# A weight block's two parts move from a raw buffer to a high-part buffer in a decoder layer on Trainium2

## The chip, the cores and the metric

The kernel runs on one core of one Trainium2 chip. The metric is the device time of one execution in microseconds (us), lower is better; the number given for a kernel is the median of its runs. Engines are named as in the profile: PE (TensorE's matmuls), PEld (its weight loads), DVE (VectorE), ACT (ScalarE), POOL (GpSimd) and SP (SyncE, which issues most DMAs).

## The reference

One layer of a hybrid decoder on 512 tokens of width 1024, in float32: RMSNorm, one input projection, a convolution branch and a gated linear attention branch, their merge, an output projection, then a channel mixer, and a last RMSNorm. The change lies in the channel mixer:

```python
u2 = _rmsnorm(h, norm2_g[l])
z = _causal_dwconv(u2 @ w_ffn_up[l], ffn_dw_w[l], ffn_dw_b[l])
h = h + (jax.nn.silu(z[..., :FFN_DIM]) * z[..., FFN_DIM:]) @ w_ffn_down[l]
```

FFN_DIM is 2816, so `w_ffn_up` is 1024 x 5632: 44 column blocks of 128. Block i (0 to 21) gives the gate of channel group i and block 22+i its value.

## The kernel before

**Three products for one.** Every float32 operand is split into a high part (the value cast to the type that TensorE multiplies, `float32r`) and a low part (the value minus its high part). One product is then three matmuls: low by high, high by low, high by high (`mm3`, L398 to L400, or `col_products`, L409).

**The flow of weights.** `order` lists all weight blocks in the order of their use. `load` (L223 issues the DMA on SP) brings the next block into a buffer of the tag "raw". `split_weight` makes its parts: ACT casts into a buffer of the tag "whi", then DVE subtracts into one of the tag "wlo" (L326 and L327 where operands are built first, L345 and L354 else). For blocks in `ADDED` the low part is made without DVE: ACT writes the negated block (L347) and POOL issues a DMA that adds the block from memory once more (L348). Each of the three tags has four buffers of 128 x 1024 floats. `prefetch(n)` splits up to n blocks ahead of the one in use; each split calls `load` once, so loads run four entries ahead.

**What orders the work.** The kernel is written with a library that plans each engine's queue and the buffers when it is built: each instruction is put into its engine's queue when a model of times has its operands and a buffer ready, earlier program text first, and a buffer passes to the next tile of its tag when the last reader of the former is done. On the chip the queues then run in that fixed order.

**Pairs in the up projection.** Channel groups come in pairs (p, q), in three lists: (0,2) (1,3) (4,6) (5,7), then (8,10) (9,11) (20,21), then (12,14) (13,15) (16,18) (17,19). After each list follows a part of the down projection (`seven("w_down", ...)`). For q in 6, 7, 10, 11, 14, 15 and 18 gate and value of q are computed together, by seven half-width products instead of eight (`up_seven`). Its four weights come from the raw blocks b (gate q) and x (value q): b itself, the sum block called "x" in the order (`up_operand`, L288, a third raw buffer), r1 called "n" and r0's right half called "m". The steps on TensorE are a11 (weight b), s1 (x), n2 (x), a12 (b), n3 (n), s4 (n), a22 (m), each of four `mm3` with 256 columns, twelve matmuls. Between them run the 24 matmuls of p's value block (block 22+p) in lots of three, one lot after a11, s1, n2 and n3, two after a12 and s4; `beside()` does this. Ahead of the pair stands p's gate, 24 matmuls on L409. ACT copies intermediate banks out for later steps: L1581 after a11, which n2 then adds to; L1584 after s1; L1587 after n2, before n3 adds to the bank; L1591 after n3, before a22. DVE forms the other half at L1593 and L1594 after s4. Then p's group goes through its depthwise convolution and gate (L1391, L1393, L1399, L1401) and is split for the down projection (L1406, L1407; L1414, L1424 to L1426 form sums).

Inside `up_seven` the next weights are split in steps: one (the next pair's gate) after n2, one (its value) after a12, one (block b of the next q) after s4, one (block x) after a22; n and m are split when `up_seven` begins.

**The lines of the change.** Block m is only 512 wide, so its high and low part share one buffer of 1024, named `wm`: ACT casts at L319, DVE subtracts at L320. In the kernel before that buffer has the tag "raw".

Of the kernel before, what the change touches and what calls it, by code (L numbers as in the profile page):

```python
# [11 lines left out]
F32R = mybir.dt.float32r  # L12
# [5 lines left out]
P = 128  # L18
D = 1024
# [60 lines left out]
def trunk_layer(ctx: ExitStack, tc: tile.TileContext, a: dict, out: bass.AP):  # L80
    nc = tc.nc

    def pool(name, bufs, space=None):
        kw = {"space": space} if space is not None else {}
        return ctx.enter_context(tc.tile_pool(name=name, bufs=bufs, **kw))
# [8 lines left out]
    wp = pool("weights", 1)  # L94
# [18 lines left out]
    def nm(s):  # L113
        return f"{s}_{next(names)}"

    def heap(dt=F32):
        return hp.tile([P, T], dt, tag="h", name=nm("h"))
# [85 lines left out]
    def load():  # L203
        if len(raws) < len(order):
            name, j = order[len(raws)]
            if name in SEVEN:
                raws.append(load_block(name, *j))
                if name in INNER and raws[-1] is None:
                    load()
                return  # L210
            raw = None
            if name == "w_up7":
                i, s = j
                name, j = "w_up", {"b": i, "x": FT + i}.get(s)
            if name == "w_r0":
                raw = raw_tile()
                for i in range(2):
                    c = slice((2 * j + i) * P, (2 * j + i + 1) * P)
                    dst = raw[:, i * T : (i + 1) * T].rearrange("p (c x) -> p c x", x=P)
                    nc.sync.dma_start(dst, a["w_r"][:4, :, c].rearrange("c p x -> p c x"))  # L220
            elif j is not None:
                raw = raw_tile()
                sent[name, j] = nc.sync.dma_start(raw, a[name.rstrip("0")][j])  # L223
            raws.append(raw)
# [50 lines left out]
    def operand(name, raw, pairs, step, d):  # L275

        if step == "s4":
            return kept[name, pairs, d, "b22"]
        if step == "n2" and name not in INNER:
            nc.vector.tensor_tensor(kept[name, pairs, d], kept[name, pairs, d], raw, ALU.add)  # L280
        return raw if step in ("a12", "n3") else kept[name, pairs, d]

    def up_operand(raw, i, s):

        if s in "bx":
            kept[i, s] = raw
        r0, r1 = kept[i, "b"], kept.get((i, "x"))
        add = lambda engine, dst, x, y: engine.tensor_tensor(dst, x, y, ALU.add)  # L288
        if s == "x":
            both = kept[i, "sum"] = raw_tile()  # L290
            add(nc.vector, both[:, :T], r0[:, :T], r1[:, :T])
            add(nc.vector, both[:, T:], both[:, :T], r1[:, T:])
            add(nc.gpsimd, r1[:, :T], r1[:, :T], r1[:, T:])
            add(nc.gpsimd, r0[:, T:], r0[:, T:], both[:, T:])
        return {"b": r0, "x": kept.get((i, "sum")), "m": r0[:, T:], "n": r1}[s]

    def sum_on(name, pairs, step, d):

        where = {"a11": (0, 1), "n2": (1, 0)}
        if name in INNER:  # L300
            where["s1"] = (1, 1)
            if (step, d) in (("s4", 0), ("s4", 1)):
                add_n3(name, pairs, d)
        if step in where:
            nxt = block(name, pairs, d, *where[step])
            nc.gpsimd.dma_start(kept[name, pairs, d], nxt, accum_op=ALU.add)

    def split_weight(between=None):
        if len(ready) < len(order):
            while len(raws) <= len(ready):  # L310
                load()
            raw = raws[len(ready)]
            name, spec = order[len(ready)]
            if name in SEVEN or name == "w_up7":
                raw = operand(name, raw, *spec) if name in SEVEN else up_operand(raw, *spec)
                n = raw.shape[-1]
                if name == "w_up7" and spec[1] == "m":
                    both = wp.tile([P, D], F32R, tag="raw", name=nm("wm"), bufs=4)
                    nc.scalar.copy(both[:, :T], raw)  # L319
                    nc.vector.tensor_tensor(both[:, T:], raw, both[:, :T].bitcast(F32), ALU.subtract)  # L320
                    ready.append((both[:, :T], both[:, T:]))
                    load()
                    return
                hi = wp.tile([P, D], F32R, tag="whi", name=nm("whi"), bufs=4)[:, :n]
                lo = wp.tile([P, D], F32R, tag="wlo", name=nm("wlo"), bufs=4)[:, :n]
                nc.scalar.copy(hi, raw)  # L326
                pace[0] = nc.vector.tensor_tensor(lo, raw, hi.bitcast(F32), ALU.subtract)  # L327
                if name in SEVEN:
                    sum_on(name, *spec)
                skipped = name in INNER and raws[len(ready)] is None  # L330
                ready.append((hi, lo))
                if not skipped:
                    load()
                return
            hi = wp.tile([P, D], F32R, tag="whi", name=nm("whi"), bufs=4)
            if order[len(ready)][0] == "w_low":
                nc.scalar.copy(hi, raw)
                if order[len(ready)][1] == 0:
                    part_lo = lambda t: t.rearrange("p (k c) -> p k c", c=P)[:, :, :RANK]
                    nc.vector.tensor_tensor(part_lo(hi), part_lo(raw), part_lo(hi.bitcast(F32)), ALU.subtract)  # L340
                ready.append((hi, None))
                load()
                return
            lo = wp.tile([P, D], F32R, tag="wlo", name=nm("wlo"), bufs=4)
            nc.scalar.copy(hi, raw)  # L345
            if order[len(ready)] in ADDED:
                pace[0] = nc.scalar.activation(lo, raw, AF.Copy, scale=-1.0)  # L347
                nc.gpsimd.dma_start(lo, a[name][spec], accum_op=ALU.add)  # L348
                ready.append((hi, lo, (name, spec) in LOW_LAST_IN))
                load()  # L350
                return
            if between:
                between()
            pace[0] = nc.vector.tensor_tensor(lo, raw, hi.bitcast(F32), ALU.subtract)  # L354
            ready.append((hi, lo))
            load()

    def prefetch(n):

        while len(ready) < min(used[0] + n, len(order)):  # L360
            split_weight()
# [821 lines left out]
    def between(h, i):  # L1183
        if h < 2:
            (glu_value if h else glu_gate)(GLU_AT[0] + GLU_AT[1] + i)
        elif h < HEADS:
            gate_b(2 * (h - 2) + i)
        else:
            gate_b(6 + i)
# [68 lines left out]
    for p, q in O_PAIRS:  # L1258

        f1 = merged(p)  # L1260
        both = heap(F32R)
# [471 lines left out]
```

## Time and profile before

| | us |
|---|---|
| median of 3 runs | 824.15 (823.98 to 824.63) |
| the profiled execution's own time | 824.73 |
| its span, first to last instruction | 823.0 |
| PE busy | 812.3 (99%) |
| DVE busy | 675.6 (82%) |
| ACT busy | 471.3 (57%) |
| POOL busy | 122.9 (15%) |

The profile is of one execution. A row of the timeline has the start (us from the span's start), the duration, the engine and source line, and what is written from what by the program's names; in brackets stands the engine's idle time before it and what ended it. Matmuls overlap in the pipeline, so their starts, not their durations, say how fast TensorE goes. A row of the waits has who waited, for whom, the total, the number of times and the longest. A row of the stretches has, after the two times and the length, the busy time of PE, PEld, DVE, ACT and POOL, each with its count, then the granted clock, the DMAs' share and GB/s.

### The profile page before, as it was taken

How to read it: one execution, taken by the hardware profiler on the slowest of the kernel's cores; microseconds unless marked ns; L12 is line 12 of the kernel's file. 1: busy time of each engine (PE TensorE's matmuls, PEld its weight loads, DVE VectorE, ACT ScalarE, POOL GpSimd, SP SyncE). 2: the span in 40 equal slices, each digit the busy share in tenths (PEclk: the TensorE clock that was granted, in tenths of full speed). 3: DMA queues.
4: the chain of work that ended last, by engine and by line, in shares of the span. 5: the costliest groups of instructions: out<-in, count | busy, mean ns of one | idle time of the engine just before them, and what ended most of it. 6: DMA issues, size and time to landing. Idle time of an engine off the chain costs nothing.

```text
span 823.0 us, 11027 instructions
## 1 busy us (share of the span) xinstructions
PE 812.3 (99%) x4090; PEld 689.9 (84%) x4090; DVE 675.6 (82%) x983; ACT 471.3 (57%) x669; POOL 122.9 (15%) x153
## 2 busy tenths in 40 slices
PE   8999999999999999999999999999999999999996
PEld 7988888888888888888888898888788888988885
DVE  6898988999988899845678859689858888588895
ACT  7663547695453552469345759554446543667455
POOL 2021101312121121000011011211021111220111
PEclk9999999999999999999999999999999999999999
DMA  9999859569666678222348459346835646557562
GB/s 328 315 319 234 199 138 225 142 154 222 149 138 143 152 191 191 81 77 79 126 110 214 148 164 222 98 122 154 217 102 149 160 92 215 154 154 203 131 128 102
DMA packets 50213, 136.65 MB, mean 166 GB/s; under 512 B 4624, under 2 KB 17184, under 8 KB 50160
## 3 DMA queue, kind: packets, MB, share of 16 engines
q1 hardware_dynamic: 37456, 90.91, 31.6%
q0 software_dynamic: 12528, 44.83, 31.4%
q8 instruction: 32, 0.52, 0.2%
q10 hardware_dynamic: 176, 0.20, 0.1%
q14 instruction: 21, 0.17, 0.1%
HBM read 133.84 MB, written 6.29 MB: 170 GB/s over the span
## 4 chain that ended last, share of the span: by engine, by line
PE 91%; DMA 3%; DVE 2%; issue 2%; ACT 1%; POOL 0%; POOLq 0%; SPq 0%; DVEq 0%; ACTq 0%
PE mm L409 52%; PE mm L399 8%; PE mm L400 8%; PE mm L398 8%; PE mm L673 2%; PE ax L398 2%; PE ax L399 2%; PE ax L400 2%; DMA wlo<-in_w_glu_dram 1%; PE ax L1147 1%; PE ax L484 1%; DMA raw<-in_w_up_dram 1%; DMA kept<-rows 1%; PE ax L1149 1%; PE ax L1129 1%
## 5 line engine op out<-in xcount | busy, mean ns | idle before, releaser
L409 PE MATMUL mm<-ul,whi 128*128 128x512 f32 (+1 forms) x608 | 226.8, 373 | 0.0
L409 PE MATMUL mm<-uh,whi 128*128 128x512 f32 (+1 forms) x608 | 226.5, 373 | 0.0
L409 PE MATMUL mm<-uh,wlo 128*128 128x512 f32 (+1 forms) x608 | 217.2, 377 | 0.3 <-DMA wlo<-in_w_glu_dram 0.2
L823 DVE SCALAR_TENSOR_TENSOR c<-h,pp,c 128x507 f32<-128x507 f32 (+20 forms) x240 | 169.9, 732 | 3.2 <-ACT c L820 0.3
L409 PEld LDWEIGHTS mm<-uh,whi 128*128 128x128 f32 x608 | 114.5, 188 | 20.4
L409 PEld LDWEIGHTS mm<-uh,wlo 128*128 128x128 f32 x608 | 114.6, 189 | 19.0 <-DMA wlo<-in_w_glu_dram 0.7
L409 PEld LDWEIGHTS mm<-ul,whi 128*128 128x128 f32 x608 | 114.8, 189 | 17.9
L345 ACT CAST whi<-raw 128x1024 fp32r<-128x1024 f32 x94 | 97.4, 1043 | 49.0 <-PE mm L409 32.0
L326 ACT CAST whi<-raw 128x1024 fp32r<-128x1024 f32 (+1 forms) x53 | 54.1, 1027 | 53.0 <-PE mm L400 29.8
L347 ACT ACTIVATE wlo<-raw 128x1024 fp32r<-128x1024 f32 x47 | 49.5, 1058 | 58.8 <-PE mm L409 54.5
L327 DVE TENSOR_TENSOR wlo<-raw,whi 128x1024 fp32r<-128x1024 f32 (+1 forms) x53 | 66.6, 1264 | 11.6 <-ACT whi L326 11.0
L1393 DVE SCALAR_TENSOR_TENSOR tmp<-mm,pp,tmp 128x511 f32<-128x511 f32 (+1 forms) x88 | 64.6, 743 | 13.2 <-ACT tmp L1391 12.8
L354 DVE TENSOR_TENSOR wlo<-raw,whi 128x1024 fp32r<-128x1024 f32 x47 | 57.0, 1220 | 16.0 <-ACT whi L345 15.6
L326 ACT CAST whi<-kept 128x1024 fp32r<-128x1024 f32 (+1 forms) x44 | 44.2, 1009 | 32.7 <-PE mm L400 10.5
L327 DVE TENSOR_TENSOR wlo<-kept,whi 128x1024 fp32r<-128x1024 f32 (+1 forms) x44 | 52.3, 1196 | 5.1 <-ACT whi L326 4.8
L1391 ACT ACTIVATE tmp<-mm,pp 128x512 f32<-128x512 f32 x44 | 33.3, 775 | 11.7 <-PE mm L409 9.7
L409 PE MATMUL mm<-h,whi 128*128 128x512 f32 x128 | 39.4, 389 | 0.0
L1313 DVE TENSOR_TENSOR hres<-hres,mm 128x512 f32<-128x512 f32 (+1 forms) x49 | 32.4, 670 | 2.5 <-PE mm L400 2.3
L348 POOL DMA_DIRECT2D wlo<-in_w_up_dram x18 | 15.6, 866 | 96.9 <-ACT wlo L347 79.0
L409 PEld LDWEIGHTS mm<-h,whi 128*128 128x128 f32 x128 | 24.0, 188 | 5.2 <-issue 0.2
L399 PE MATMUL mm<-wlo,sh 128*128 128x512 f32 x66 | 25.9, 393 | 0.0
L400 PE MATMUL mm<-whi,sh 128*128 128x512 f32 x66 | 25.7, 390 | 0.0
(366 smaller groups left out, 1649.1 us busy)
## 6 DMA issues: line engine op xcount, KB each, us to landing
raw<-in_w_up_dram SPq DMA_DIRECT2D x44, 512.0 KB, 4.6
wlo<-in_w_up_dram POOLq DMA_DIRECT2D x18, 512.0 KB, 7.8
raw<-in_w_glu_dram SPq DMA_DIRECT2D x16, 512.0 KB, 5.6
raw<-in_w_down_dram SPq DMA_DIRECT2D x15, 512.0 KB, 5.2
kept<-in_w_down_dram POOLq DMA_DIRECT2D x10, 512.0 KB, 5.4
raw<-in_w_v_dram SPq DMA_DIRECT2D x8, 512.0 KB, 6.4
rows<-in_w_r_dram SPq DMA_DIRECT2D x16, 256.0 KB, 5.9
raw<-in_w_qk_dram SPq DMA_DIRECT2D x8, 512.0 KB, 4.0
```

The costliest lines, as they stand in the source:

```text
L326: nc.scalar.copy(hi, raw)
L327: pace[0] = nc.vector.tensor_tensor(lo, raw, hi.bitcast(F32), ALU.subtract)
L345: nc.scalar.copy(hi, raw)
L347: pace[0] = nc.scalar.activation(lo, raw, AF.Copy, scale=-1.0)
L354: pace[0] = nc.vector.tensor_tensor(lo, raw, hi.bitcast(F32), ALU.subtract)
L398: nc.tensor.matmul(acc, ll, rh, start=first, stop=False, **kw)
L399: nc.tensor.matmul(acc, lh, rl, start=False, stop=False, **kw)
L400: nc.tensor.matmul(acc, lh, rh, start=False, stop=last, **kw)
L409: nc.tensor.matmul(acc[:, lo:hi], l, r, start=n == 0, stop=n == len(todo) - 1)
L823: nc.vector.scalar_tensor_tensor(y[:, s:], c[:, : T - s], w, y[:, s:], ALU.mult, ALU.add)
L1391: nc.scalar.activation(z, acc, AF.Identity, bias=pp[:, PP_FB + m : PP_FB + m + 1], scale=w[2])
L1393: nc.vector.scalar_tensor_tensor(z[:, s:], acc[:, : T - s], w[j], z[:, s:], ALU.mult, ALU.add)
```

## The change

One word: the buffer of `wm` takes the tag "whi" instead of "raw". Nothing else in the text is touched; the cast and the subtraction stay as they are.

```diff
                 if name == "w_up7" and spec[1] == "m":
-                    both = wp.tile([P, D], F32R, tag="raw", name=nm("wm"), bufs=4)
+                    both = wp.tile([P, D], F32R, tag="whi", name=nm("wm"), bufs=4)
                     nc.scalar.copy(both[:, :T], raw)
                     nc.vector.tensor_tensor(both[:, T:], raw, both[:, :T].bitcast(F32), ALU.subtract)
                     ready.append((both[:, :T], both[:, T:]))
                     load()
                     return
```

A pair by seven products has so far used six raw buffers (gate and value of p, b, x, the sum, `wm`) and five high buffers (gate and value of p, b, x, n); after the change it uses five raw and six high ones, out of four of each.

## The prediction

> **What bounds the kernel now.** I read the page first, then the waits of TensorE's weight loads for the stretch with the pairs by seven products (505 to 770 us), then single stretches of the timeline. From the page:
>
> ```profile
> span 823.0 us, 11027 instructions
> PE 812.3 (99%) x4090; PEld 689.9 (84%) x4090; DVE 675.6 (82%) x983; ACT 471.3 (57%) x669; POOL 122.9 (15%) x153
> PE 91%; DMA 3%; DVE 2%; issue 2%; ACT 1%; POOL 0%; POOLq 0%; SPq 0%; DVEq 0%; ACTq 0%
> ```
>
> TensorE fills 99% of the span and 91% of the chain. A change of buffers removes no matmul, so all that it can win is what TensorE waits in the stages that it touches. The waits of the weight loads say how little that is:
>
> ```profile
> PEld ax L398 <- ACT mm L1587: 1.9, 4, 0.9
> PEld ax L398 <- ACT mm L1581: 1.4, 1, 1.4
> PEld mm L399 <- DVE wlo L327: 0.7, 2, 0.3
> PEld mm L398 <- ACT whi L326: 0.6, 1, 0.6
> ```
>
> The first two belong to the pairs: ScalarE's copies out of a bank that the next step adds to. One long wait for L1581, one of 0.9 and three that share 1.0 for L1587. The last two are of the down projection. Two waits, then, are worth looking at; both stand in pair (5, 7):
>
> ```profile
> 547.45 0.40 PE L409 MATMUL mm<-ul,whi 128*128 128x512 f32 x1
> 547.69 0.39 PE L409 MATMUL mm<-uh,whi 128*128 128x512 f32 x1
> 549.00 0.39 PE L398 MATMUL ax<-n,wlo 128*128 128x256 f32 x1 [0.92 <-ACT mm L1581]
> ...
> 553.82 0.39 PE L409 MATMUL mm<-uh,whi 128*128 128x512 f32 x1
> 554.66 0.38 PE L398 MATMUL ax<-n3h,wlo 128*128 128x256 f32 x1 [0.45 <-ACT mm L1587]
> ```
>
> Matmuls of 512 columns start 0.24 apart (547.45 to 547.69). The next starts come 1.31 and 0.84 later, so TensorE loses 1.07 before step n2 and 0.60 before step n3: 1.67 us. That, with at most 1.0 in other pairs, is the whole prize.
>
> Why were those copies late? ScalarE in that pair:
>
> ```profile
> 544.00 0.62 ACT L319 CAST wm<-raw 128x512 fp32r<-128x512 f32 x1 [2.35 <-DVE wlo L327]
> 546.59 0.63 ACT L1399 ACTIVATE tmp<-tmp 128x512 f32<-128x512 f32 x1 [1.96 <-DVE tmp L1393]
> 547.12 0.61 ACT L1406 CAST yh<-w 128x512 fp32r<-128x512 f32 x1
> 547.63 1.05 ACT L326 CAST whi<-raw 128x1024 fp32r<-128x1024 f32 x1
> 548.58 0.36 ACT L1581 COPY mm<-ax 128x256 f32<-128x256 f32 x1
> ...
> 551.64 1.05 ACT L326 CAST whi<-kept 128x1024 fp32r<-128x1024 f32 x1
> 553.50 0.83 ACT L1406 CAST sh<-v 128x768 fp32r<-128x768 f32 x1 [0.82 <-DVE v L1426]
> 554.24 0.36 ACT L1587 ACTIVATE mm<-ax 128x256 f32<-128x256 f32 x1
> ```
>
> Both copies stand behind work that waits for VectorE (L1393, L1426), so VectorE is behind. Its backlog begins in the pair before:
>
> ```profile
> 531.12 0.69 DVE L320 TENSOR_TENSOR wm<-raw,wm 128x512 fp32r<-128x512 f32 x1 [3.62 <-ACT wm L319]
> 537.60 0.69 DVE L288 TENSOR_TENSOR raw<-raw,raw 128x512 f32<-128x512 f32 x1 [5.79 <-DMA raw<-in_w_up_dram]
> ```
> ```profile
> 531.84 0.33 SPq L223 DMA_DIRECT2D raw<-in_w_up_dram  x1
> ```
>
> VectorE idles 5.79 us until block x of pair 7 lands. That load is issued 0.03 after L320 ends (531.12 + 0.69 = 531.81): it takes the raw buffer of block b of pair 6, which L320 reads last. So the parts of block m are on the path, and what holds them is a buffer:
>
> ```profile
> 528.29 1.06 ACT L347 ACTIVATE wlo<-raw 128x1024 fp32r<-128x1024 f32 x1
> 529.25 1.03 ACT L345 CAST whi<-raw 128x1024 fp32r<-128x1024 f32 x1
> 530.19 0.36 ACT L1587 ACTIVATE mm<-ax 128x256 f32<-128x256 f32 x1
> 530.49 0.60 ACT L319 CAST wm<-raw 128x512 fp32r<-128x512 f32 x1
> 531.00 1.05 ACT L345 CAST whi<-raw 128x1024 fp32r<-128x1024 f32 x1
> ```
>
> L319 runs when weight 5 has been split (L347, L345): only then is a raw buffer free. Weight 5's parts wait in turn for step n2 to let go of block x's parts:
>
> ```profile
> 528.21 0.28 PE L400 MATMUL ax<-n,whi 128*128 128x256 f32 x1
> ...
> 530.34 0.28 PE L400 MATMUL mm<-uh,whi 128*128 128x256 f32 x1
> ...
> 531.84 0.28 PE L398 MATMUL ax<-n3h,wlo 128*128 128x256 f32 x1
> ...
> 535.25 0.28 PE L400 MATMUL mm<-s,whi 128*128 128x256 f32 x1
> ...
> 536.76 0.28 PE L398 MATMUL mm<-uh,wm 128*128 128x256 f32 x1
> ...
> 538.07 0.28 PE L400 MATMUL mm<-uh,wm 128*128 128x256 f32 x1
> ```
>
> These are the last matmuls of n2 and a12, the first of n3, the last of s4, the first and last of a22.
>
> **The change part by part.** No instruction is added, and the cast and subtraction of m keep their shape (0.60 and 0.69). What changes is who holds which buffer.
>
> Raw side: a pair takes five raw buffers instead of six. Block m no longer waits for weight 5 to be split.
>
> High side: a pair takes six of the four high buffers instead of five, so each owner gets the buffer that is let go one step later. In pair (4, 6): m takes the one freed by n2 (528.21), weight 5 the one by a12 (530.34, was n2), weight 22+5 the one by s4 (535.25, was a12), block b of 7 the one after s4's companions, at 536.76 (was 535.25), block x of 7 the one of m itself, freed by a22 (538.07, was about 535 to 537). None is needed early: after a22 stands a gate of 24 matmuls before b's first product, in the chain of another pair
>
> ```profile
> 621.23 5.47 PE mm L409 x24
> ```
>
> 5.47 us, and cast and subtraction take 1.05 + 1.2.
>
> First term, block x of 7 earlier. L347 still goes first (its low buffer is freed earlier); then L319 takes the place of L345 at 529.25 and ends at 529.85, L320 ends near 530.6, and the load leaves there instead of at 531.84: 1.2 us earlier. No other issue stands on SP's queue from 526 to 534 in that view, so it overtakes none. VectorE's backlog starts 1.2 earlier. L1581 then ends at 548.94 - 1.2 = 547.7 against the 547.93 at which TensorE wants it: the wait of 1.07 goes. L1587, late by 0.60, would end 1.2 earlier, but TensorE comes 1.07 earlier too: late by about 0.5. If L320 of pair 7 (0.69), which moves behind n2, falls behind L1426, the rest goes too. Bounds 0.1 and 0.6; I take 0.3.
>
> Second term, the three small waits for L1587 in later pairs, 0 to 1.0. The weight load that waited 1.4 cost TensorE 1.07, the one of 0.9 cost 0.60: about 0.3 less each time. Three of 0.33 then cost about 0.1, and I take that.
>
> Third term, a loss. The first two high buffers of the down projection move as well: its second weight is now cast after s4 of pair (5, 7) and its subtraction comes behind L1593.
>
> ```profile
> 556.13 1.23 DVE L327 TENSOR_TENSOR wlo<-kept,whi 128x1024 fp32r<-128x1024 f32 x1
> 558.57 0.43 DVE L1593 TENSOR_TENSOR mm<-att,ax 128x256 f32<-128x256 f32 x1 [1.22 <-PE mm L400]
> ```
> ```profile
> 559.50:582.00 22.50, 22.31 (x103) 17.89 (x102) 22.11 (x30) 11.49 (x15) 2.57 (x3) 1.00 0.71 163
> ```
>
> Before, that 1.23 filled time in which VectorE then still idled 1.22 for s4. Behind s4 VectorE is busy 22.11 of 22.50 us (the third busy column), and the waits for L327 and L326 shown above are its. So 0 to 1.23 come back; nothing says which weight TensorE would take meanwhile, so I take the middle, 0.6.
>
> Sum: -1.07 - 0.3 - 0.1 + 0.6 = -0.87 us. The profiled execution took 824.73 us (span 823.0 and 1.7 around it), so it would take 823.9; the median of the three runs is 0.58 lower, and from it, 824.15 - 0.87 = **823.3**.
>
> **The rivals.** *Full relief*: VectorE's order bends so that the third term is nothing and L1587 is free: -1.07 - 0.60 and half of the small waits' 1.0 = -2.2, 822.0. For it: TensorE took other weights' products elsewhere without a gap; against it: VectorE's 22.11 of 22.50.
>
> *Nothing moves*: weight 5's cast, not m's, gets the buffer that n2 frees. Then m gets a12's at 530.34, runs at about the same time as before, and the time stays 824.2. For it: the cast of 5 was ready at that moment as well. Against it: m stands earlier in the program.
>
> *Slower*: ScalarE's order stays, while its casts now wait. Before, the cast of 22+5 (531.00) and its negated copy L347 stand ahead of L1591, the copy that a22 adds to. If they stay there, the cast starts only when s4 ends, at 535.57 (0.32 after its last matmul), L347 about 0.95 later, and L1591 ends near 537.9 instead of 533.8; a22 wants it at 536.76. That is 1.2 us in each of the six pairs whose next weight has its low part made by L347. It outweighs the gain from one such pair and passes 0.2% from three on (3.6 - 0.9 = +2.7, 826.8); with six, 7.2 - 0.9 = +6.3, 830.4. Against it: the order in the queues was made with the buffers' times in view, since L347 (low part) runs before L345 (high part) of the same weight.
>
> The Trainium skill, TensorE: Matmul & The Clock Gate, Architectural detail, says that ScalarE's and VectorE's queues are strictly first in, first out. The trace agrees: L1581 started only at 548.58, behind a cast that began at 547.63. By that rule a late cast blocks every copy behind it, which is this rival. The Trainium skill, Perfetto Trace Analysis, Optimization Strategy, reads a gap that repeats on the busy engine as a sign of too few buffers; here the gaps do not repeat (1.07 once, 0.60 once), so that rule does not yet speak of the high buffers.
>
> **How the numbers follow.** Forecast 0.44, full relief 0.26, nothing moves 0.06, slower 0.24. A measurement of this kernel can tell about 0.2% (1.65 us) from no change: below 822.5 lie full relief and a small part of the forecast, 0.28; above 825.8 the slower case, 0.24; between, 0.48. The forecast's own range, from the bounds of its terms (-1.07 - 0.60 - 0.1 + 0 and -1.07 - 0.1 - 0 + 1.23), is 822.4 to 824.2. For 8 in 10 the range takes in full relief with the whole 1.0 of the small waits (824.15 - 2.7 = 821.4) and the slower case to about three or four pairs (827.5).
>
> **What would show it.** Right: L319 of pair 6 near 529.3, the load of x near 530.6, no gap before n2 of pair (5, 7), a longer wait near 567 to 581. Wrong: L345 or L326 waiting at ScalarE for a PE step with L1587 or L1591 behind it and a gap before n3 or a22 in several pairs; or L319 still behind L345.

## The result and the profile after

| | us | ratio to the kernel before [95%] |
|---|---|---|
| kernel before, median of 9 runs | 824.39 (823.31 to 826.73) | |
| kernel after, median of 9 runs | 826.61 (825.89 to 828.8) | 1.0026 [1.0015, 1.0037] |
| the profiled execution of after | 828.11 | |

The changed kernel is slower by 0.26%, about 2.2 us. The page of after answers to the three lines quoted first in the prediction:

```profile
span 826.4 us, 11029 instructions
...
PE 815.0 (99%) x4090; PEld 692.1 (84%) x4090; DVE 674.7 (82%) x983; ACT 470.1 (57%) x669; POOL 123.8 (15%) x153
...
PE 84%; DVE 6%; DMA 5%; issue 3%; ACT 1%; POOL 0%; POOLq 0%; ACTq 0%; DVEq 0%
```

As many matmuls as before; but TensorE's share of the chain fell from 91% to 84%, VectorE's rose from 2% to 6%, the DMAs' from 3% to 5%. The span is 3.4 us longer. Not all of it belongs to the change. Up to 505 us the queues of the two kernels hold the same instructions in the same order, and yet the same matmul (`mm<-uh,whi`, the last ahead of a short wait) starts here in the timeline of before and here in that of after:

```profile
505.78 0.39 PE L409 MATMUL mm<-uh,whi 128*128 128x512 f32 x1
```
```profile
507.46 0.39 PE L409 MATMUL mm<-uh,whi 128*128 128x512 f32 x1
```

So this execution of after brings 1.68 us along (nearly all of it from the first ten microseconds), and 3.37 - 1.68 = 1.7 us are the change's own. In what follows 1.68 is taken off where times of the two are compared. Matching the matmuls one by one gives where those 1.7 us arise:

| stretch | after minus before, us |
|---|---|
| pair (5, 7) | -1.91 |
| down projection of the first list | +1.71 |
| from there to step s1 of pair (13, 15) | -0.23 |
| pair (13, 15) | +1.44 |
| pair (16, 18) | +0.73 |

**The first two rows are what the prediction described.** ScalarE in pair (4, 6) and the load of block x, from the timeline of after:

```profile
529.92 1.06 ACT L347 ACTIVATE wlo<-raw 128x1024 fp32r<-128x1024 f32 x1
530.88 0.60 ACT L319 CAST wm<-raw 128x512 fp32r<-128x512 f32 x1
531.39 0.36 ACT L1587 ACTIVATE mm<-ax 128x256 f32<-128x256 f32 x1
...
535.08 0.36 ACT L1591 COPY mm<-ax 128x256 f32<-128x256 f32 x1 [1.03 <-PE ax L400]
537.20 1.05 ACT L345 CAST whi<-raw 128x1024 fp32r<-128x1024 f32 x1 [1.76 <-PE mm L400]
538.59 0.78 ACT L1391 ACTIVATE tmp<-mm,pp 128x512 f32<-128x512 f32 x1 [0.34 <-PE mm L409]
539.26 1.04 ACT L326 CAST whi<-raw 128x1024 fp32r<-128x1024 f32 x1
```
```profile
532.24 0.33 SPq L223 DMA_DIRECT2D raw<-in_w_up_dram  x1
```

L319 runs at 530.88 - 1.68 = 529.2, the load leaves at 530.6: the two signs, to 0.1 us. L1587 and L1591 stand ahead of the casts that wait. The cast of block 22+5 (L345) waits 1.76 us for s4, and block b of 7 (L326) comes after the companions: the order of owners that the prediction wrote down.

**The last two rows are what it did not.** The waits of TensorE's weight loads in after, from 505 to 775 us:

```profile
PEld ax L398 <- ACT mm L1581: 1.8, 2, 1.2
PEld ax L398 <- ACT mm L1587: 1.3, 2, 0.7
PEld mm L399 <- DVE wlo L327: 1.3, 2, 1.0
PEld mm L398 <- DVE yl L1407: 1.0, 1, 1.0
PEld mm L398 <- ACT whi L326: 0.8, 2, 0.6
PEld ax L399 <- DVE wlo L327: 0.4, 1, 0.4
...
```

The last four belong to down projections (the row left out, 0.4, stands in before too). The first two are the pairs': the same two copies as before, L1581 and L1587, only that the waits no longer stand in pair (5, 7) but in (13, 15) and (16, 18). Take VectorE between s4 of pair (12, 14) and the next pair, first before, then after:

```profile
711.77 0.43 DVE L1594 TENSOR_TENSOR mm<-att,mm 128x256 f32<-128x256 f32 x1
712.32 1.23 DVE L327 TENSOR_TENSOR wlo<-raw,whi 128x1024 fp32r<-128x1024 f32 x1
713.47 0.74 DVE L1393 SCALAR_TENSOR_TENSOR tmp<-mm,pp,tmp 128x511 f32<-128x511 f32 x1
714.12 0.68 DVE L288 TENSOR_TENSOR raw<-raw,raw 128x512 f32<-128x512 f32 x1
```
```profile
712.96 0.43 DVE L1594 TENSOR_TENSOR mm<-att,mm 128x256 f32<-128x256 f32 x1
715.59 1.42 DVE L288 TENSOR_TENSOR raw<-raw,raw 128x512 f32<-128x512 f32 x2 [2.20 <-ACT whi L326]
716.92 0.74 DVE L1393 SCALAR_TENSOR_TENSOR tmp<-mm,pp,tmp 128x511 f32<-128x511 f32 x1
717.58 1.66 DVE L327 TENSOR_TENSOR wlo<-raw,whi 128x1024 fp32r<-128x1024 f32 x1
```

Before, VectorE goes from s4's sums straight to block b's subtraction (L327 at 712.32), then to the group's convolution (L1393), then to the sum for x (L288). After, it idles 2.20 us and does the sum first; b's subtraction starts 4.62 us after L1594 (712.96 to 717.58) instead of 0.55 (711.77 to 712.32). The reason stands in ScalarE's queue of after, and so does the price:

```profile
712.43 1.05 ACT L345 CAST whi<-raw 128x1024 fp32r<-128x1024 f32 x1 [1.76 <-PE mm L400]
713.81 0.78 ACT L1391 ACTIVATE tmp<-mm,pp 128x512 f32<-128x512 f32 x1 [0.34 <-PE mm L409]
714.49 1.04 ACT L326 CAST whi<-raw 128x1024 fp32r<-128x1024 f32 x1
...
723.33 0.62 ACT L1406 CAST yh<-w 128x512 fp32r<-128x512 f32 x1 [3.82 <-DVE w L1414]
723.85 1.05 ACT L326 CAST whi<-raw 128x1024 fp32r<-128x1024 f32 x1
725.33 0.36 ACT L1581 COPY mm<-ax 128x256 f32<-128x256 f32 x1
```
```profile
724.54 0.39 PE L409 MATMUL mm<-uh,whi 128*128 128x512 f32 x1
725.75 0.39 PE L398 MATMUL ax<-n,wlo 128*128 128x256 f32 x1 [0.82 <-ACT mm L1581]
```

The buffer that s4 frees goes to weight 22+13 (L345, 712.43), and block b of 15 gets the next one, behind L1391 (714.49). VectorE ends its backlog late, ScalarE waits 3.82 us for it at L1406, and L1581, two places behind L1406, comes too late for n2: the next start is 1.21 us after the last, 0.98 more than a matmul of 512 columns takes. That is the chain which the prediction had read in pair (5, 7), now in another pair.

### The profile page after: what moved, and what is told of

It reads as the page before. It is cut to its first block, busy times and chain, and to the rows that moved or that the text cites. A ratio compares the mean times of both kernels' runs of the same rounds, so it can differ in the third digit from the quotient of the medians.

```text
span 826.4 us, 11029 instructions
## 1 busy us (share of the span) xinstructions
PE 815.0 (99%) x4090; PEld 692.1 (84%) x4090; DVE 674.7 (82%) x983; ACT 470.1 (57%) x669; POOL 123.8 (15%) x153
## 4 chain that ended last, share of the span: by engine, by line
PE 84%; DVE 6%; DMA 5%; issue 3%; ACT 1%; POOL 0%; POOLq 0%; ACTq 0%; DVEq 0%
PE mm L409 49%; PE mm L399 7%; PE mm L400 7%; PE mm L398 7%; PE mm L673 2%; DVE tmp L1393 2%; DMA raw<-in_w_up_dram 2%; PE ax L398 2%; PE ax L399 2%; PE ax L400 2%; DMA wlo<-in_w_glu_dram 1%; PE ax L484 1%; PE ax L1147 1%; DVE wlo L327 1%; DMA kept<-rows 1%
## 5 line engine op out<-in xcount | busy, mean ns | idle before, releaser
L345 ACT CAST whi<-raw 128x1024 fp32r<-128x1024 f32 x94 | 97.3, 1044 | 55.9 <-PE mm L409 32.0
L327 DVE TENSOR_TENSOR wlo<-raw,whi 128x1024 fp32r<-128x1024 f32 (+1 forms) x53 | 69.5, 1320 | 11.1 <-ACT whi L326 11.0
L326 ACT CAST whi<-raw 128x1024 fp32r<-128x1024 f32 (+1 forms) x53 | 53.7, 1025 | 40.8 <-PE mm L400 21.6
L1393 DVE SCALAR_TENSOR_TENSOR tmp<-mm,pp,tmp 128x511 f32<-128x511 f32 (+1 forms) x88 | 64.1, 743 | 15.7 <-ACT tmp L1391 15.3
L326 ACT CAST whi<-kept 128x1024 fp32r<-128x1024 f32 (+1 forms) x44 | 44.3, 1009 | 34.8 <-PE mm L400 10.4
L327 DVE TENSOR_TENSOR wlo<-kept,whi 128x1024 fp32r<-128x1024 f32 (+1 forms) x44 | 52.3, 1197 | 5.2 <-ACT whi L326 4.9
L1391 ACT ACTIVATE tmp<-mm,pp 128x512 f32<-128x512 f32 x44 | 33.2, 773 | 15.1 <-PE mm L409 15.1
```

The source lines that it names most:

```text
L1391: nc.scalar.activation(z, acc, AF.Identity, bias=pp[:, PP_FB + m : PP_FB + m + 1], scale=w[2])
L1393: nc.vector.scalar_tensor_tensor(z[:, s:], acc[:, : T - s], w[j], z[:, s:], ALU.mult, ALU.add)
```

## The experiments

Each of the times below stands beside runs of the kernel before on the same chip (824.28, 824.10 and 824.49 us in three groups). In every diff the line is that of `wm`, unless it says otherwise.

**One group alone: 6.** Its block m frees the raw buffer for pair (5, 7).

```diff
-both = wp.tile([P, D], F32R, tag="raw", name=nm("wm"), bufs=4)
+both = wp.tile([P, D], F32R, tag="whi" if spec[0] in (6,) else "raw", name=nm("wm"), bufs=4)
```

> Only pair (4, 6) puts block m's parts into a high buffer; the other six pairs keep the raw one. Main theory: the whole change won about 1.8 us in pair (5, 7), because the load of block x of 7 leaves earlier, and lost it in other places, each by the high buffers that m of another pair takes (the down projection behind pair (5, 7), pairs (13, 15) and (16, 18)). Then this is 1.5 to 1.9 us faster than before, with no gap before n2 and n3 in pair (5, 7) and none new elsewhere. Rival, loads: the early load of block x itself does the harm later on, by taking the DMA engines from other loads: then the down projection behind (5, 7) still loses some 1.5 us and the sum is near 0.

Measured: 822.69 us (822.13 to 824.54), ratio 0.9983 [0.9974, 0.9991], -1.6 us. The three longest waits that are left between 505 and 775 us (the two left out, 0.4 and 0.3, stand in before too):

```profile
PEld ax L398 <- ACT mm L1587: 1.0, 3, 0.3
PEld mm L399 <- DVE wlo L327: 0.7, 2, 0.3
PEld mm L398 <- ACT whi L326: 0.6, 1, 0.6
...
```

L1581's wait of 1.4 is gone, the longest for L1587 fell from 0.9 to 0.3, and no new row came. So the first term of the prediction (-1.37) holds by itself in sign and place, and the earlier load of block x of 7 does no harm behind it. That the size fits too is in part luck, as the account below shows.

**High buffer taken, raw buffer not given back.** The high part goes into a high buffer, the low part into a raw one.

```diff
-both = wp.tile([P, D], F32R, tag="whi", name=nm("wm"), bufs=4)
-nc.scalar.copy(both[:, :T], raw)
-nc.vector.tensor_tensor(both[:, T:], raw, both[:, :T].bitcast(F32), ALU.subtract)
+hi = wp.tile([P, D], F32R, tag="whi", name=nm("wm"), bufs=4)[:, :T]
+lo = wp.tile([P, D], F32R, tag="raw", name=nm("wm"), bufs=4)[:, :T]
+nc.scalar.copy(hi, raw)
+nc.vector.tensor_tensor(lo, raw, hi.bitcast(F32), ALU.subtract)
```

> Block m's high part goes into a high buffer and its low part into a raw one, so that m takes one of each: the high buffers turn as after the change, the raw ones as before. Main theory (the loss is the high buffers' later release): no gain in pair (5, 7), the losses stay, so 1.5 to 3.5 us slower than before. Rival, loads (the loss comes from raw blocks loaded earlier, which meet other transfers): raw loads leave as before, so within 0.3 us of before.

Measured: 830.06 us (828.84 to 832.28), 1.0069 [1.0054, 1.0084], +5.8 us, more than any theory had said. The rival's condition was not met, so this run does not decide between the two: the raw loads do not leave as before. Block m's low part takes a raw buffer, and VectorE waits 5.00 us for weight 5 to be cast, which now comes late, before it writes that part; so the load of block x of 7 leaves at 533.24 instead of 531.84, and that of 15 is 1.4 us later too. The size comes from a wait that neither kernel has (the two longest rows; source lines stand one lower here):

```profile
PEld ax L399 <- DVE wlo L328: 4.9, 3, 2.7
PEld ax L399 <- ACT mm L1582: 1.4, 1, 1.4
...
```

Step s1 waits three times for the subtraction of block x: the casts are late as after, x's load is later than in either kernel, and both delays meet on VectorE. The two sides of the change do not simply add.

**A buffer of its own.** `wm` takes neither kind; it gets one buffer apart. The room for it comes from three pad tiles (352, 2016 and 768 bytes a partition) which nothing reads or writes and which are left out; the run beside it is the kernel before without those pads.

```diff
-    for i, part in enumerate((cp, edge)):
-        part.tile([P, PADS[i] // 4], F32, name=nm("pad"))
...
-both = wp.tile([P, D], F32R, tag="raw", name=nm("wm"), bufs=4)
+both = fp.tile([P, D], F32R, tag="wm", name=nm("wm"), bufs=1)
...
-    tp.tile([P, PADS[2] // 4], F32, name=nm("pad"))
```

> Block m's parts take a buffer of their own; raw buffers turn as after the change (five a pair), high ones as before (five a pair). Room for it comes from leaving out three unused pads, which shifts addresses (the next run is the kernel before without the pads). Main theory: gain without loss, 1.5 to 2.2 us faster than the kernel before without the pads, no gaps in the pairs. Rival, loads: the raw blocks are loaded as early as after the change, so the same losses, 1 to 2.5 us slower.

> The kernel before without its three unused pads, the reference for the kernel with a buffer of its own: the order of every queue is the one of before, only addresses differ. Both theories: within 0.3 us of before. If it differs by more, addresses cost or win time by themselves, and the private buffer is to be read against this run alone.

Measured: 824.80 us (823.5 to 826.09), 1.0000 [0.999, 1.001], with the own buffer; 826.68 us (824.83 to 828.62), 1.0026 [1.0016, 1.0037], for the kernel before without pads. The difference between the two is -1.9 us; against the kernel before the own buffer alone shows nothing. All waits of TensorE's weight loads in the own buffer's trace from 505 to 775 us (source lines two to three lower):

```profile
PEld mm L397 <- DVE wlo L325: 0.6, 2, 0.3
PEld mm L396 <- ACT whi L324: 0.6, 1, 0.6
PEld mm L407 <- DMA wlo<-in_w_up_dram: 0.2, 1, 0.2
```

No pair waits for a copy any more, and the down projection waits as in the kernel before. The raw relief without the sixth owner of a high buffer has the gain and none of the losses. That is the half of the change which helps, shown apart from the half which costs. (The two versions without pads share the slower stretch described at the end, so it falls out of their difference.)

**The other groups in parts.** The same edit as for group 6, with (14, 15, 18), then (7,), then (10, 11).

> Only the three pairs of the last list (q = 14, 15, 18) put block m into a high buffer. Main theory: the next pair's block b is cast one release later, VectorE stands at the sum for block x, and copies L1581 and L1587 come late in pairs (13, 15) and (16, 18); 1.3 to 2.2 us slower than before, with gaps before n2 and n3 in those two pairs only. Rival, chance order: the losses of the whole change come from how its effects in the earlier lists shift the later queues; then within 0.5 us of before.

> Only pair (5, 7) puts block m into a high buffer. Main theory: the first two weights of the down projection are cast and split later (their sums with them), while nothing is won in the pair; 1.0 to 2.0 us slower than before, gaps in the down projection near 567 to 583. Rival, chance order: within 0.5 us of before.

> Only the pairs of the middle list (q = 10, 11). In the trace of the whole change this stretch lost nothing. Main theory and rival: within 0.5 us of before; with the other three single runs the four parts should sum to the whole change, about +2.2 us, if they do not act on each other.

| groups with the high buffer | median, us | ratio [95%] | against before, us |
|---|---|---|---|
| 14, 15, 18 | 825.36 | 1.0012 [1.0004, 1.0021] | +1.26 |
| 7 | 826.45 | 1.0025 [1.0014, 1.0037] | +2.35 |
| 10, 11 | 823.86 | 0.9993 [0.9983, 1.0003] | -0.24 |
| all seven | 826.61 | 1.0026 [1.0015, 1.0037] | +2.2 |

With group 6 the parts add up to -1.6 + 2.35 - 0.24 + 1.26 = +1.8, near the whole; each part is known to 0.7 to 1.0 us only, so the agreement can't be read more finely than that. The loss of 14, 15 and 18 came out a little below what was expected; in its trace the new gaps stand in pairs (13, 15) and (16, 18) alone. That of 7 came out above: its trace shows only 1.0 us more in the down projection, and its profiled execution (825.62) is among the quickest of its eight (825.04 to 827.24). Where the rest of the 2.35 arises no trace here shows; the interval allows anything from about 1.2 to 3.0.

**The sum for x behind block b's subtraction.** If the loss were only that VectorE stands at the head of its queue for the sum, an order in which b's subtraction goes first would mend it. An edit of the changed kernel, in `up_operand`:

```diff
-add(nc.vector, both[:, :T], r0[:, :T], r1[:, :T])
+with tc.issue_after(pace[0].ins): add(nc.vector, both[:, :T], r0[:, :T], r1[:, :T])
```

> The whole change, and in addition VectorE's first sum for block x is put behind the subtraction of block b in its queue, so that VectorE has other work while block x is still on its way. Main theory in its narrow form (the loss in the pairs is VectorE standing at the sum, at the head of its queue): the gaps before n2 and n3 in pairs (13, 15) and (16, 18) go, the loss in the down projection stays; 1.2 to 2.0 us faster than the whole change, so 0 to 1 us slower than before. Rival, late cast: it is the late cast of block b itself that delays what follows, whatever the order; then no faster than the whole change.

Measured: 829.63 us (828.23 to 830.42), 1.0058 [1.0045, 1.0071], 3.0 us slower than the changed kernel. VectorE there, after s4 of pair (12, 14), and the wait that results:

```profile
714.53 0.43 DVE L1594 TENSOR_TENSOR mm<-att,mm 128x256 f32<-128x256 f32 x1
716.19 1.54 DVE L1393 SCALAR_TENSOR_TENSOR tmp<-mm,pp,tmp 128x511 f32<-128x511 f32 x2 [1.24 <-ACT tmp L1391]
717.64 1.21 DVE L327 TENSOR_TENSOR wlo<-raw,whi 128x1024 fp32r<-128x1024 f32 x1
...
719.38 0.68 DVE L288 TENSOR_TENSOR raw<-raw,raw 128x512 f32<-128x512 f32 x1
```
```profile
PEld ax L398 <- DVE wlo L327: 4.6, 4, 1.3
...
PEld mm L409 <- DMA wlo<-in_w_up_dram: 1.2, 3, 0.6
```

b's subtraction stands ahead of the sum again, but it cannot start ahead of its cast (L326, 716.06 to 717.10), so the sum comes at 719.38 and x's subtraction is late for s1, four times. The gaps before n2 and n3 went; gaps before s1 took their place. In pairs (13, 15) and (16, 18) this order is even the better one in the trace, 1.3 us lost instead of 2.2. But it loses 1.2 us in each of the pairs (5, 7) and (9, 11), where the planned order lost nothing, and the gates behind three pairs now wait for the DMA that adds to their low part. So the theory that the order alone costs has fallen: with the late cast either order loses, and over all pairs the one that was planned loses less.

**Groups 6, 10 and 11; group 14 alone.** The same edit, with (6, 10, 11) and with (14,).

> The high-part buffer is given to the fourth block of groups 6, 10 and 11 alone; 7, 14, 15 and 18 keep the raw one. Theory (the parts of the change add up, each acting through the buffers of the next pair): the -1.6 us of group 6 alone and the -0.2 us of 10 and 11 alone add up to about -1.8 us against the kernel before (between -1.0 and -2.5), with no gap before n2 and n3 of pair (5, 7) and none in the later pairs or the down projection beyond those of the kernel before. Rival (a moved buffer shifts every later one, so the sum of parts does not hold): no gain, -0.5 to +2.5 us, with new gaps in the second or third list.

> The high-part buffer is given to the fourth block of group 14 alone. Theory (the next pair's block b gets its high buffer later, and nothing beyond): gaps before n2 and n3 of pair (13, 15) alone, 0.3 to 1.4 us in sum, none in (16, 18), so +0.3 to +1.4 us. Rival (the loss in (13, 15) comes from group 15's own buffer, or is spread): no gap in (13, 15), change within 0.3 us of the kernel before.

Measured: 823.10 us (821.95 to 823.98), 0.9981 [0.9973, 0.999], for 6, 10 and 11. That is -1.4 us by the medians and -1.6 by the ratio, near the sum of the parts, so the rival of that run falls. This version and that with group 6 alone (0.9983) beat both kernels; the runs do not tell the two apart. Group 14 alone: 824.72 us (823.07 to 825.91), 1.0004 [0.9995, 1.0012]. Its time can't be told from that of before and lies just under what was expected, but its profiled execution (825.91) is the slowest of twelve and shows the mechanism as expected: gaps in pair (13, 15), 1.6 us in sum, and none that is new in (16, 18). It also shows what sets their size. VectorE's row of the sum and TensorE's first matmul of n2, for group 14 alone:

```profile
713.59 1.42 DVE L288 TENSOR_TENSOR raw<-raw,raw 128x512 f32<-128x512 f32 x2 [1.84 <-DMA raw<-in_w_up_dram]
```
```profile
723.76 0.39 PE L398 MATMUL ax<-n,wlo 128*128 128x256 f32 x1 [0.48 <-ACT mm L1581]
```

And VectorE's row of the sum for groups 14, 15 and 18:

```profile
713.21 1.42 DVE L288 TENSOR_TENSOR raw<-raw,raw 128x512 f32<-128x512 f32 x2 [1.40 <-DMA raw<-in_w_up_dram]
```

The three kernels with this order let VectorE idle 1.40, 1.84 and 2.20 us for the sum, and lose 0.19, 0.64 and 0.98 us before n2. Each tenth that block x's load lands later is a tenth lost before n2, so in this order the pair hangs on a DMA (the gap before n3, 0.32, 0.85 and 0.32, does not follow it). (The row of after names L326, which ended at the same moment; in the other two the sum starts while that cast still runs, so L326 does not hold it.)

That load has a share in the loss which the late cast does not explain. In the three kernels it leaves 1.2 us earlier than in before, since L320 comes earlier, and takes 7.2, 7.65 and 8.0 us to land; in the six traces whose order in this pair is that of before it takes 5.4 to 6.0. So it lands no earlier for leaving earlier. An estimate from these rows, tenth for tenth: had it taken 6.0 us, the gap before n2 would not have arisen even with the late cast. What makes it longer was not tried, so a collision of the earlier load with other transfers is not excluded for this part of the loss.

## Why the prediction was wrong

**Bounds and first term: right.** Two waits in pair (5, 7) were the prize, block m's raw buffer held them, and the sixth owner of a raw buffer was the cause. After shows -1.9 us there against the -1.37 forecast, and group 6 alone -1.6 in the runs. One detail differs: the load of x took 6.42 us from issue to use instead of 5.76. The adding DMA for block 22+5 now leaves earlier too; whether it is the cause was not tried. The 1.3 us gained at the issue became 0.6 at the landing. ScalarE still reached L1406 2.1 us earlier (546.66 - 1.68 against 547.12), because the planned order changed too. On VectorE two instructions of L1393 instead of four stand between the sum and L1414, whose result L1406 casts, so L1414 starts at 546.21 - 1.68 = 544.53 instead of 546.42; on ScalarE L1399, which stood ahead of L1406 and waited 1.96 us, now comes behind L1581. That is why both waits went, and not only the first.

The size owes something to luck. The prediction took its prize from one execution. Five of the traces have the order of before in pair (5, 7), and the same matmuls (545.56 to 556.06 in before) take longer there than with group 6's order by 1.9 us (before itself), 1.3, 1.0, 0.65 and 0.6: 1.1 on average. The interval of group 6's runs, about -2.1 to -0.7 us, holds that as well as the forecast.

**Third term: right in place, too small.** +0.6 was forecast with 1.23 as the upper bound; the down projection lost 1.7. It was bounded by one subtraction that moves. Two weights moved: the first one's cast came later as well (555.28 - 1.68 = 553.60, in before 551.64), and with it the DMA that adds to its raw copy, for which ScalarE then waited 2.21 us instead of 0.74. VectorE, behind it, comes late to L1407, and TensorE waits:

```profile
563.53 1.05 ACT L326 CAST whi<-kept 128x1024 fp32r<-128x1024 f32 x1 [2.21 <-DMA kept<-in_w_down_dram]
```
```profile
568.16 0.50 PE L398 MATMUL mm<-whi,yl 128*128 128x512 f32 x1 [0.57 <-DVE yl L1407]
```

The matmul ahead of it starts at 567.21, 0.95 us earlier, so this wait costs 0.7 us. Group 7 alone, which wins nothing in pair (5, 7), does not have it and loses 1.0 here: so 0.7 of the 1.9 won in the pair is given back because TensorE comes earlier and VectorE does not come as much earlier. From 567 us on the planned order of some of TensorE's own matmuls changes too, in each kernel with group 7's m in a high buffer; what that alone costs was not tried. (One of the two waits for L327 which the prediction counted here, 0.3, is of the second list's down projection; both kernels have it.)

**The failed step: "None is needed early", with the second term that rests on it.** The high side was written down owner by owner, and correctly. Its cost was then judged by TensorE alone: 5.47 us of another gate stand between a22 and b's first product, so a cast 1.5 us later seemed free. But TensorE is not the first that needs block b. VectorE's subtraction of b was what it did while x's load was still under way; without b it had nothing to do, idled 2.20 us and did the subtraction later, in the midst of the convolution on which L1406 and then L1581 wait. The load of x, which also took longer, decides how large that idle time is. The second term promised 0.1 us from the later pairs; pairs (13, 15) and (16, 18) lost 2.2 in the trace, and groups 14, 15 and 18 alone lose 1.26 in the runs. The rule that the prediction applied to the second weight of the down projection (a subtraction that filled idle time of VectorE) had to be applied to block b of each pair.

**The rivals.** *Full relief* fell with that step. *Nothing moves* fell on L319 at 530.88. *Slower* came true in its sign and not in its mechanism: it had L1587 and L1591 wait behind a cast, but in the rows of pair (4, 6) both stand ahead of the casts that wait. Its point of decision (three pairs at 1.2 us) has nothing to do with what happened.

The Trainium skill, Perfetto Trace Analysis, Optimization Strategy, takes a gap that repeats on the busy engine as a sign of too few buffers. After the change it does speak: the gaps before n2 and n3 stand in two pairs one after the other, and they disappear with the buffer of its own (no row for L1581 or L1587 in that trace). The Trainium skill, TensorE: Matmul & The Clock Gate, Architectural detail, has VectorE's queue strictly first in, first out. The 2.20 us in front of the sum agree: the convolution step L1393 behind the sum had its input from L1391 at 714.59, a full 1.0 us before the sum began.

**What stays open.** Why group 7 alone costs 2.35 us in its runs where its trace shows 1.0; why x's load takes 7.2 to 8.0 us when it leaves earlier; and the share of the 2.2 us that varies from execution to execution with the landing of x. The own buffer with the pads kept was not tried.

## What to carry to other kernels

A buffer that moves from one pool to another gives all later owners in the second pool a place one release later; write down who gets which, and then ask of each delayed tile which engine touches it first, not when the bound engine needs it. Work that fills an engine's idle time while it waits for a transfer has a due time as well: the moment at which that idle time begins. Where a change acts in several places, run it place by place: here one of seven places carried the gain (-1.6 us), and others that looked the same carried the loss.

## What the runs showed of the hardware

**Addresses alone moved the time.** The kernel before without its pads has the same queues in the same order, and takes 2.4 us more (1.0026 [1.0016, 1.0037]). The stretch from 88 to 430 us of before, then of the kernel without pads (the columns are as in the prediction's rows of stretches):

```profile
88.00:430.00 342.00, 342.00 (x1575) 285.25 (x1574) 288.98 (x433) 188.64 (x260) 46.91 (x57) 1.00 0.60 148
```
```profile
88.00:430.00 342.00, 342.00 (x1566) 283.93 (x1565) 288.54 (x433) 188.16 (x259) 47.27 (x57) 1.00 0.58 147
```

TensorE is busy throughout at the same granted clock, and does nine matmuls fewer in the same time, about 2 us. The own buffer, also without pads, has 1566 too; the other kernels have 1573 to 1575. Which tile's address it is was not tried.

**A gap can belong to the execution.** In the kernel without pads and in that of groups 14, 15 and 18, whose order in pair (5, 7) is that of before, the gap of 1.07 us before n2 is nearly gone, because block x landed earlier. One profiled execution tells where a wait can arise, not how much of it every run has.
